# Turning tiles by VectorE's squares of 32 and ScalarE's copies instead of TensorE's transposes, in a hybrid mLSTM and RWKV-7 decoder layer on one core

## The chip, the core and the metric

The kernel runs on one core of a Trainium2 chip. A core has TensorE (PE, matrix products, results in PSUM), VectorE (DVE), ScalarE (ACT), GpSimd (POOL) and SyncE (SP, which here only starts DMAs). The engines run side by side, each through its own list of instructions in order, and wait for one another by semaphores. The metric is the time on the device for one execution, in microseconds (us).

## What is computed

One decoder layer for 256 tokens of width 2048, all in float32. Cut to what matters here:

```python
def hybrid_mixer(h, ...):
    proj = h @ w_in                                   # 2048 -> mLSTM, RWKV and gate columns
    q, k, v, o, ir, fr = split_cols(mlstm_p, MLSTM_COLS)
    hm = mlstm_chunkwise(q, k, v, ig, logf)           # 4 heads, values of 256
    hm = hm * lax.rsqrt(jnp.mean(hm * hm, -1, keepdims=True) + RMS_EPS) * head_norm
    ha = jax.nn.sigmoid(o) * hm
    rp = rwkv_p + (shift_right(rwkv_p, 1) - rwkv_p) * mu
    r, kr, vr, wl, al, gl = split_cols(rp, RWKV_COLS)
    y = rwkv7_scan(r_h, heads(decay), kr, v_h, kk, kk * a_h)   # 16 heads of 64
    y = (y - mean) * lax.rsqrt(var + RWKV_GN_EPS) * per_head(ln_g) + per_head(ln_b)
    y = y + jnp.sum(r_h * kr * r_k, -1, keepdims=True) * v_h
    hb = y.reshape(B, S, RWKV_WIDTH) * g
    merged = sigmoid(g_a) * (ha @ w_branch_a) + sigmoid(g_b) * (hb @ w_branch_b)
    return merged @ w_out

x = x + rms_norm(hybrid_mixer(rms_norm(x)), ...)
x = x + rms_norm(cross_attention(rms_norm(x), rms_norm(mem)), ...)
x = x + rms_norm(conv_glu_ffn(rms_norm(x)), ...)
```

## The kernel before

All large products run through one list of blocks (`block`, `run`). A block is 512 output columns of one weight matrix (1024 in the last). Its weights come in tiles of 512 KB, 128 x 1024 numbers, by SP's queue. Each tile is split in two parts for precision: ScalarE casts it to `wh` (L410), VectorE subtracts to get `wl` (L432), and TensorE makes three products, `xh*wh`, `xl*wh` and `xh*wl`, into PSUM tiles called `fm` (features on partitions) or `tm` (tokens on partitions). A `fm` tile of weights is 24 matmuls of 128x256. There are three buffers for `raw`, four each for `wh` and `wl`.

Counted from 0, tiles 0 to 7 are the small columns, 8 to 71 RWKV's r, k, v and mLSTM's q, k, 72 to 103 mLSTM's v and o as `tm`, 104 to 111 and 112 to 119 the first two gate blocks, then branch and gate blocks in turn (120 to 123 is the first branch block on `ha`, 168 to 171 the first on `hb`), and after them the mixer's output, cross-attention and the feed-forward part, which is most of the span.

All other work is side work, written as Python generators and dealt out between the matmuls by a class `Spread`. `side.half()` is called at every half tile. It runs a piece (up to the next `yield`) of the first bulk generator or of a back one if a budget for VectorE and ScalarE allows it, and a piece of each chain whose turn it is: a chain with `chain=3` comes every third half tile. `side.need(s)` runs a generator to its end at once. Before each block, `run` needs the evacuation of the block before the last:

```python
            if len(pend) >= 2:
                side.need(pend[-2])
```

The order on each engine is fixed by this when the program is built (a manual schedule).

The pieces that the change touches: `gates` (chain of 1) makes mLSTM's gate row `R[6]` and spreads it over 128 partitions by matmuls with a row of the identity (`gbc`, from a split copy `g2`), for `pw`. `v_evac` makes RWKV's v in features (`vT`) and turns it into tokens (`vt`) by TensorE's transposes. `rwkv` (both halves `together`, a chain of 3) runs four chunks of 64 tokens; in chunks 0 to 2 it turns the keys BK into `bkt`, then come the steps gram, lv1 with X, lv2, U, and Tn with Y; after chunks 1 and 3 the outputs are normed (`gm`, `gv`) and turned (`yT`) into `z`. `mlstm`, the tail of the evacuation of the last `o` block, makes its output `so` in tokens and turns it (`haT`) for the split into `ha`. `hb_split` makes `hb` from RWKV's outputs with the products `zg`, whose weights `gwh` and `gwl` it splits twice; `need_hb` needs it before the first branch block on `hb`. `x_tokens`, in the feed-forward part, already turns x by VectorE's transpose of squares of 32 (`xq`) and sixteen ScalarE copies of 32 partitions (`xt`) that put the squares into their places.

Of the kernel before, what the change touches and what calls it, by code (L numbers as in the profile page):

```python
# [9 lines left out]
F32 = mybir.dt.float32  # L10
F32R = mybir.dt.float32r
# [141 lines left out]
def _layer(ctx, tc, nc, d, dbg):  # L153
# [58 lines left out]
    E2 = [slice(0, 64), slice(64, 128)]  # L212
    mhalf = cp.tile([P, 16], F32, name="mhalf")
    pool.memset(mhalf, -0.5)
# [439 lines left out]

    id4 = cp.tile([4, 4], F32R, name="id4")

    def gates():

        act.copy(id4, con[0:4, 0:4])
        RT = M["rows"]  # L660
# [72 lines left out]
        M["pw"] = pw  # L733
        g2 = T2("g2", dt=F32R)
        split(g2[0:4, 0], g2[0:4, 1], R[6])
        for _ in range(6):
            yield
        for h2 in range(2):
            q = aux("gbc", [P, 2, S])
            for j in range(2):  # L740
                sel = id4[:, h2 * 2 + j:h2 * 2 + j + 1].broadcast_to((4, P))
                mm(q[:, j], sel, g2[0:4, 0], stop=False)
                mm(q[:, j], sel, g2[0:4, 1], start=False)
            for j in range(2):
                h = h2 * 2 + j
                for (jt, dq), ci in CI.items():
                    o = jt * 256 + dq * 64 - jt * 128
                    dve.tensor_scalar(pw[:, h, o:o + 64], q[:, j, dq * 64:(dq + 1) * 64], cols[:, ci, h:h + 1], 0.0,
                                      op0=ALU.subtract, op1=ALU.max)
                yield  # L750
# [171 lines left out]
    def v_evac(hf):  # L922
        def gen(ps):
            if hf == 0:
                M["vT"], M["vt"] = U("vT"), U("vt", [P, 2, 1024])
            for g in range(2):
                p0 = hf * 4 + g * 2
                pr = PR()
                dve.tensor_mul(pr, ps[g], bc(st0.rb, 2))
                yield  # L930
                for j in range(2):
                    shiftmix(M["vT"][:, p0 + j], pr[:, j], 16 + p0 + j)
                yield
            for _ in range(4):
                yield
            for t in range(2):
                q = aux("vt", [P, 4, 128])
                for j in range(4):
                    pe.transpose(q[:, j], M["vT"][:, hf * 4 + j, t * P:(t + 1) * P], ident)
                act.copy(M["vt"][:, t, hf * 512:(hf + 1) * 512], q)  # L940
                yield
            M["v", hf] = True
            start_rwkv()
            tasks["bon", hf] = side.add(bonus(hf), back=True)
        return gen

    def bonus(hf):
# [11 lines left out]
    def rwkv(hf):  # L959
# [6 lines left out]
        def heads():  # L966
            for j in range(4):
                for e in range(2):
                    yield j, e

        ysb = None
        for c in range(4):
# [5 lines left out]
            if c < 3:  # L978
                q = aux("bkt", [P, 4, 128])
                for j in range(4):  # L980
                    pe.transpose(q[:, j], flat(BK[:, p0 + j, c]), ident)
                act.copy(bkt, q)
                yield
            au = C("au", f"au{hf}", [P, 2, 2, 4, 64])
# [15 lines left out]
            for e in range(2):  # L1000
                act.copy(uv[E2[1 - e], e], v[:, e])
            yield

# [9 lines left out]
            if c:  # L1013
                q = aux("X0", [P, 4, 64])
                for j, e in heads():
                    mm(q[E2[e], j], KR[E2[e], p0 + j, c, 0], T[hf][E2[e], j])
                for e in range(2):
                    dve.tensor_add(uv[E2[e], e], uv[E2[e], e], q[E2[e]])
            yield
            q = aux("lv2", [P, 4, 32])  # L1020
            for j, e in heads():
                mm(q[e * 64:e * 64 + 32, j], t1[E2[e], j], mt[E2[e], j, 32:64])
            for e in range(2):
                r = slice(e * 64, e * 64 + 32)
                dve.tensor_copy(mt[r, :, 32:64], q[r])
            yield
            q = aux("U", [P, 4, 64])
# [49 lines left out]
            dve.tensor_mul(y, y, r.unsqueeze(2).broadcast_to((P, 8, 64)))  # L1077
            yield
            yield
            q = aux("yT", [P, 4, 128])  # L1080
            for j in range(4):
                pe.transpose(q[:, j], y[:, j * 2:j * 2 + 2].rearrange("p a b -> p (a b)"), ident)
            z = bg[:, 1].rearrange("p (j t) -> p j t", j=4)
            for j in range(4):
                act.activation(z[:, j], q[:, j], AF.Identity, scale=pcol("lng", p0 + j), bias=pcol("lnb", p0 + j))
            yield
# [55 lines left out]
    def mlstm():  # L1142
# [4 lines left out]
        for t in range(2):  # L1147
# [12 lines left out]
            for h2 in range(2):  # L1160
# [19 lines left out]
                yield  # L1180
        ha = [U(f"ha{i}", dt=F32R) for i in range(2)]
        M["ha"] = ha
        for k2 in range(4):
            q = aux("haT", [P, 2, S])
            for j in range(2):
                k = k2 * 2 + j
                for t in range(2):
                    pe.transpose(q[:, j, t * P:(t + 1) * P], so[:, t, k * P:(k + 1) * P], ident)
# [476 lines left out]
    def x_tokens():  # L1665

        M["xt"] = []
        for f in range(4):
            if f % 2 == 0:
                M["xt"].append(U("xt", [P, 2, 1024]))  # L1670
            q = C("xq", f"au{f % 2}", [P, 4, 2, 4, 32])
            flat = q.rearrange("p k t b i -> p (k t b i)")
            for i in range(2):
                v = M["xr"][f // 2][:, f % 2 * 4 + i * 2:f % 2 * 4 + i * 2 + 2]
                dve.transpose(flat[:, i * 512:(i + 1) * 512], v.rearrange("p k s -> p (k s)"))
                yield
            o = M["xt"][f // 2][:, :, f % 2 * 512:f % 2 * 512 + 512].rearrange("p t (k b i) -> p t k b i", k=4, b=4)
            for b in range(4):
                for c in range(4):
                    act.copy(o[b * 32:b * 32 + 32, :, :, c], q[c * 32:c * 32 + 32, :, :, b].rearrange("p k t i -> p t k i"))  # L1680
                    if c % 2:
                        yield

# [157 lines left out]
```

## Time and profile before

| what | value |
|---|---|
| median of 3 runs | 1883.01 us (1882.06 to 1885.18) |
| the profiled execution | 1882.86 us |
| its span in the profile | 1881.1 us |
| TensorE busy | 1867.8 us (99%) |
| VectorE busy | 1313.9 us (70%) |
| ScalarE busy | 1035.0 us (55%) |
| GpSimd busy | 30.6 us (2%) |
| mean granted TensorE clock | 0.997 |

How to read the profile: a row of groups has line, engine, operation, tiles written and read, shapes and count, then the busy time, the mean of one in ns, the idle time of the engine just before, and what ended it. A row of a tile has the count, then the shortest, median and longest duration. A row of the timeline has the start in us, the time from the first start to the last end of the instructions merged in it, the engine, the instruction and their count; in brackets stands idle time before it and its releaser. A row of windows has the stretch, its length, the busy time (and instructions) of PE, PE's weight loads, DVE, ACT and POOL, the granted TensorE clock, and the share and rate of the DMA engines. A row of waits has who waited for whom, total, times, longest. Nearly all operations of the side work are recorded at L66, in a helper that meters them, and plain matmuls at L188.

Matmuls are pipelined: the durations of neighbours overlap, so their distance in the timeline says what one costs in a stream. In some matmul groups a few records are missing.

### The profile page before, as it was taken

To read this page: it belongs to the slowest core of one execution; us is meant where nothing else is said; L and a number is where in the kernel's file an instruction comes from. 1 tells how busy PE (TensorE), PEld (TensorE's weight loads), DVE (VectorE), ACT (ScalarE), POOL (GpSimd) and SP (SyncE) were. 2 spreads that over 40 slices of the span, in tenths; PEclk is the share of its full clock that TensorE was granted. 3 is DMA by queue.
4 is the path that set the end of the run, shared out by engine and by line. 5 is a ranking of instruction groups with operands and counts; after the bars stand their busy time and mean duration, and the time that the engine had idled before them with its cause. 6 is when DMAs were issued, how large, how long until landed. Compare 5 with 4: busy or idle time off the path is not lost.

```text
span 1881.1 us, 36660 instructions
## 1 busy us (share of the span) xinstructions
PE 1867.8 (99%) x15038; PEld 1774.5 (94%) x15038; DVE 1313.9 (70%) x1957; ACT 1035.0 (55%) x1619; POOL 30.6 (2%) x53
## 2 busy tenths in 40 slices
PE   9999999999999999999999999999999999999998
PEld 9999988999999999899999999999999998888886
DVE  6879985765765767777877666777666675556555
ACT  6677355554544655666565555564445555545453
POOL 0000000100100000000000000000000000000000
PEclk9999999999999999999999999999999999999999
DMA  7655554354556664545555566555655556555554
GB/s 252 196 175 181 167 177 146 110 175 146 182 175 206 237 234 163 176 163 180 197 196 192 199 194 198 194 191 191 195 198 193 196 191 216 195 192 196 193 190 154
DMA packets 97912, 352.73 MB, mean 188 GB/s; under 512 B 11056, under 2 KB 11312, under 8 KB 97360
## 3 DMA queue, kind: packets, MB, share of 16 engines
q1 hardware_dynamic: 96496, 348.07, 56.2%
q8 instruction: 117, 1.92, 0.4%
q0 software_dynamic: 384, 1.18, 0.3%
q10 hardware_dynamic: 864, 1.15, 0.2%
q14 instruction: 51, 0.42, 0.1%
HBM read 347.73 MB, written 2.10 MB: 186 GB/s over the span
## 4 chain that ended last, share of the span: by engine, by line
PE 95%; DVE 3%; issue 1%; ACT 1%; DMA 0%; POOL 0%; SPq 0%; DVEq 0%; POOLq 0%; ACTq 0%
PE fm L188 66%; PE tm L188 24%; DVE wl L432 1%; PE gram L188 0%; PE Y L188 0%; DVE ql L66 0%; ACT wh L410 0%; PE lv L188 0%; DMA wsm<-in_w_sm_dram 0%; DVE z L66 0%; PE num L188 0%; DVE hl L66 0%; PE X L188 0%; PE zwa L188 0%; PE U L188 0%
## 5 line engine op out<-in xcount | busy, mean ns | idle before, releaser
L432 DVE TENSOR_TENSOR wl<-raw,wh 128x1024 fp32r<-128x1024 f32 (+2 forms) x756 | 789.3, 1059 | 427.4 <-ACT wh L410 424.3
L410 ACT CAST wh<-raw 128x1024 fp32r<-128x1024 f32 (+2 forms) x756 | 679.8, 916 | 520.7 <-PE fm L188 335.0
L188 PE MATMUL fm<-fh,wl 128*128 128x256 f32 x2048 | 566.3, 277 | 0.5 <-DVE wl L432 0.4
L188 PE MATMUL fm<-fh,wh 128*128 128x256 f32 x2048 | 566.3, 277 | 0.1
L188 PE MATMUL fm<-fl,wh 128*128 128x256 f32 x2048 | 565.0, 276 | 0.0
L188 PEld LDWEIGHTS fm<-fh,wl 128*128 128x128 f32 x2048 | 385.0, 188 | 1.0 <-DVE wl L432 1.0
L188 PEld LDWEIGHTS fm<-fh,wh 128*128 128x128 f32 x2048 | 384.9, 188 | 0.4 <-ACT fh L66 0.4
L188 PEld LDWEIGHTS fm<-fl,wh 128*128 128x128 f32 x2048 | 384.5, 188 | 0.0
L188 PE MATMUL tm<-wh,as 128*128 128x512 f32 x1024 | 315.1, 389 | 0.0
L188 PE MATMUL fm<-hh,wh 128*128 128x256 f32 x1072 | 302.0, 282 | 1.4 <-ACT wh L421 1.4
L188 PE MATMUL fm<-hh,wl 128*128 128x256 f32 x1072 | 298.3, 278 | 0.1
L188 PE MATMUL fm<-hl,wh 128*128 128x256 f32 x1072 | 298.2, 278 | 0.0
L188 PEld LDWEIGHTS tm<-wh,as 128*128 128x128 f32 x1024 | 192.1, 188 | 39.8
L188 PEld LDWEIGHTS fm<-hh,wh 128*128 128x128 f32 x1072 | 202.4, 189 | 3.4 <-ACT hh L66 1.5
L188 PEld LDWEIGHTS fm<-hl,wh 128*128 128x128 f32 x1072 | 202.4, 189 | 0.2
L188 PEld LDWEIGHTS fm<-hh,wl 128*128 128x128 f32 x1072 | 202.3, 189 | 0.3 <-DVE wl L422 0.3
L188 PE MATMUL tm<-wl,as 128*128 128x512 f32 x512 | 199.2, 389 | 0.0
L188 PEld LDWEIGHTS tm<-wl,as 128*128 128x128 f32 x512 | 96.1, 188 | 20.0
L66 ACT CAST as<-ac 128x256 fp32r<-128x256 f32 x128 | 45.6, 404 | 113.5 <-PE tm L188 113.5
L66 DVE TENSOR_TENSOR as<-ac,as 128x256 fp32r<-128x256 f32 x128 | 48.6, 421 | 62.2 <-ACT as L66 62.2
L188 PE MATMUL fm<-mgh,wh 128*128 128x256 f32 x256 | 71.0, 277 | 0.0
L188 PE MATMUL fm<-mgh,wl 128*128 128x256 f32 x256 | 70.9, 277 | 0.0
(361 smaller groups left out, 2156.1 us busy)
## 6 DMA issues: line engine op xcount, KB each, us to landing
raw<-in_w_fu_dram SPq DMA_DIRECT2D x256, 512.0 KB, 4.2
raw<-in_w_in_dram SPq DMA_DIRECT2D x160, 512.0 KB, 3.7
raw<-in_w_fd_dram SPq DMA_DIRECT2D x128, 512.0 KB, 4.0
raw<-in_w_br_dram SPq DMA_DIRECT2D x32, 512.0 KB, 3.9
raw<-in_w_mo_dram SPq DMA_DIRECT2D x32, 512.0 KB, 4.1
raw<-in_w_xk_dram SPq DMA_DIRECT2D x8, 512.0 KB, 4.3
raw<-in_w_xq_dram SPq DMA_DIRECT2D x8, 512.0 KB, 3.6
raw<-in_w_xv_dram SPq DMA_DIRECT2D x8, 512.0 KB, 3.9
```

The lines of the kernel that those rows point to most:

```text
L66: return f(out, *a, **k)
L188: pe.matmul(out, lhsT, rhs, start=start, stop=stop, skip_group_check=True)
L410: nc.scalar.copy(h, v)
L432: nc.vector.tensor_sub(l, v, h)
```

## The change

Four transposes and one spreading by TensorE are replaced. A helper `turned` (taken out of `x_tokens`) and two like it (`squares`, `h_features`) transpose squares of 32 on VectorE and move the squares on ScalarE. v becomes a chain of its own (`v_tokens`, every second half tile); the keys' copies are dealt out, three per half of the heads, over the steps of a chunk; the outputs' copies go four at a time over the recurrence's steps; mLSTM's output goes through an extra tile `hs`, its first token tile as a chain beside the second. The gates' row goes to 128 partitions by four DMAs from POOL's queue into `gb`, with eight turns of waiting instead of six. The T2 tiles get a seventh buffer.

```diff
-        return mp.tile(shape or [P, 2, S], dt, tag="T2", bufs=6, name=name)
+        return mp.tile(shape or [P, 2, S], dt, tag="T2", bufs=7, name=name)
...
+    def turned(q, v, o):
+        n = v.shape[1]
+        flat = q.rearrange("p k t b i -> p (k t b i)")
+        for k in range(0, n, 2):
+            dve.transpose(flat[:, k * S:(k + 2) * S], v[:, k:k + 2].rearrange("p k s -> p (k s)"))
+            yield
+        o = o.rearrange("p t (k b i) -> p t k b i", k=n, b=4)
+        for b in range(4):
+            for c in range(4):
+                act.copy(o[b * 32:b * 32 + 32, :, :, c], q[c * 32:c * 32 + 32, :, :, b].rearrange("p k t i -> p t k i"))
+                if c % 2:
+                    yield
...
-        g2 = T2("g2", dt=F32R)
-        split(g2[0:4, 0], g2[0:4, 1], R[6])
-        for _ in range(6):
+        gb = C("gb", "au1", [P, 4, S])
+        for h in range(4):
+            pool.dma_start(gb[:, h], R[6][h:h + 1].unsqueeze(1).broadcast_to((1, P, S)))
+        for _ in range(8):
             yield
         for h2 in range(2):
-            q = aux("gbc", [P, 2, S])
-            for j in range(2):
-                sel = id4[:, h2 * 2 + j:h2 * 2 + j + 1].broadcast_to((4, P))
-                mm(q[:, j], sel, g2[0:4, 0], stop=False)
-                mm(q[:, j], sel, g2[0:4, 1], start=False)
...
-            for t in range(2):
-                q = aux("vt", [P, 4, 128])
-                for j in range(4):
-                    pe.transpose(q[:, j], M["vT"][:, hf * 4 + j, t * P:(t + 1) * P], ident)
-                act.copy(M["vt"][:, t, hf * 512:(hf + 1) * 512], q)
-                yield
...
+            side.add(v_tokens(hf), chain=2)
...
+        def squares(o, v):
+            q = T2("bq", [P, 4, 4, 32])
+            dve.transpose(q.rearrange("p j b i -> p j (b i)"), v)
+            yield
+            for b in range(4):
+                for a in range(4):
+                    act.copy(o[b * 32:b * 32 + 32, :, a * 32:a * 32 + 32], q[a * 32:a * 32 + 32, :, b])
+                    yield
...
-                q = aux("bkt", [P, 4, 128])
-                for j in range(4):
-                    pe.transpose(q[:, j], flat(BK[:, p0 + j, c]), ident)
-                act.copy(bkt, q)
-                yield
+                turn = squares(bkt, BK[:, p0:p0 + 4, c].rearrange("p j s t -> p j (s t)"))
+                next(turn)
...
+                for _ in zip(range(3), turn):
+                    pass
                 yield
...
-            yield
-            q = aux("yT", [P, 4, 128])
+            z = bg[:, 1].rearrange("p (j t) -> p j t", j=4)
+            turn = squares(z, y.rearrange("p (j e) v -> p j (e v)", e=2))
+            next(turn)
+            yield
+            for n in range(16):
+                next(turn)
+                if n % 4 == 3:
+                    yield
...
+            if t == 0:
+                hs = U("hs", [P, 2, 8, 4, 32])
+                turn0 = side.add(h_features(hs[:, 0], so[:, 0]), chain=1)
+        yield from h_features(hs[:, 1], so[:, 1])
+        side.need(turn0)
...
-            q = aux("haT", [P, 2, S])
             for j in range(2):
                 k = k2 * 2 + j
-                for t in range(2):
-                    pe.transpose(q[:, j, t * P:(t + 1) * P], so[:, t, k * P:(k + 1) * P], ident)
-            for j in range(2):
-                k = k2 * 2 + j
-                split_gain(ha[0][:, k], ha[1][:, k], q[:, j], pcol("hn", k))
+                h, l = (v[:, k].rearrange("p (t s) -> p t s", t=2) for v in ha)
+                split_gain(h, l, sof[:, k], pcol("hn", k))
             yield
+    def h_features(q, v):
+        flat = q.rearrange("p k b i -> p (k b i)")
+        for i in range(2):
+            dve.transpose(flat[:, i * 512:(i + 1) * 512], v[:, i * 512:(i + 1) * 512])
+            yield
+        o = v.rearrange("p (k a i) -> p k a i", k=8, a=4)
+        for b in range(4):
+            for a in range(4):
+                act.copy(o[b * 32:b * 32 + 32, :, a], q[a * 32:a * 32 + 32, :, b])
+                if a % 2:
+                    yield
```

More of the change, by code (lines that the diff above doesn't have):

```diff
@@ L212, in _layer @@
     E2 = [slice(0, 64), slice(64, 128)]
-    mhalf = cp.tile([P, 16], F32, name="mhalf")
+    mhalf = cp.tile([P, 24], F32, name="mhalf")
     pool.memset(mhalf, -0.5)
@@ L933, in gen, with v_tokens @@
                 yield
-            for _ in range(4):
-                yield
-            for t in range(2):
-                q = aux("vt", [P, 4, 128])
-                for j in range(4):
-                    pe.transpose(q[:, j], M["vT"][:, hf * 4 + j, t * P:(t + 1) * P], ident)
-                act.copy(M["vt"][:, t, hf * 512:(hf + 1) * 512], q)
-                yield
-            M["v", hf] = True
-            start_rwkv()
-            tasks["bon", hf] = side.add(bonus(hf), back=True)
-        return gen
+            side.add(v_tokens(hf), chain=2)
+        return gen
+    def v_tokens(hf):
+        for p0 in (hf * 4, hf * 4 + 2):
+            yield from turned(T2("vq", [P, 2, 2, 4, 32]), M["vT"][:, p0:p0 + 2], M["vt"][:, :, p0 * P:p0 * P + 256])
+        M["v", hf] = True
+        start_rwkv()
+        tasks["bon", hf] = side.add(bonus(hf), back=True)
     def bonus(hf):
@@ L978, in rwkv @@
             if c < 3:
[L979 to L983 removed]
+                turn = squares(bkt, BK[:, p0:p0 + 4, c].rearrange("p j s t -> p j (s t)"))
+                next(turn)
+            else:
+                turn = iter(())
             au = C("au", f"au{hf}", [P, 2, 2, 4, 64])
@@ L1001, in rwkv @@
                 act.copy(uv[E2[1 - e], e], v[:, e])
+            for _ in zip(range(3), turn):
+                pass
             yield
@@ L1018, in rwkv @@
                     dve.tensor_add(uv[E2[e], e], uv[E2[e], e], q[E2[e]])
+            for _ in zip(range(3), turn):
+                pass
             yield
@@ L1025, in rwkv @@
                 dve.tensor_copy(mt[r, :, 32:64], q[r])
+            for _ in turn:
+                pass
             yield
@@ L1078, in rwkv @@
             yield
+            z = bg[:, 1].rearrange("p (j t) -> p j t", j=4)
+            turn = squares(z, y.rearrange("p (j e) v -> p j (e v)", e=2))
+            next(turn)
             yield
-            q = aux("yT", [P, 4, 128])
+            for n in range(16):
+                next(turn)
+                if n % 4 == 3:
+                    yield
             for j in range(4):
[L1082 to L1085, printed above, removed]
+                act.activation(z[:, j], z[:, j], AF.Identity, scale=pcol("lng", p0 + j), bias=pcol("lnb", p0 + j))
             yield
@@ L1671, in x_tokens @@
             q = C("xq", f"au{f % 2}", [P, 4, 2, 4, 32])
[L1672 to L1675, printed above, removed]
+            v = M["xr"][f // 2][:, f % 2 * 4:f % 2 * 4 + 4]
+            o = M["xt"][f // 2][:, :, f % 2 * 512:f % 2 * 512 + 512]
+            for _ in turned(q, v, o):
                 yield
[L1677 to L1682, printed above, removed]
     def load_gain():
```

5 lines of the change are left out of this document (2 added, 3 removed).

## The prediction

> **What bounds the kernel now.** I read the page first, then who waited for whom, then the order of time around the places that the change touches.
>
> ```profile
> span 1881.1 us, 36660 instructions
> PE 1867.8 (99%) x15038; PEld 1774.5 (94%) x15038; DVE 1313.9 (70%) x1957; ACT 1035.0 (55%) x1619; POOL 30.6 (2%) x53
> PE 95%; DVE 3%; issue 1%; ACT 1%; DMA 0%; POOL 0%; SPq 0%; DVEq 0%; POOLq 0%; ACTq 0%
> ```
>
> TensorE (PE) is busy for 99% of the span and is 95% of the chain that ended last. So every microsecond taken out of its stream is a microsecond won, as long as nothing else makes it wait. What could is the staging of the weights: ScalarE casts each 512 KB tile (wh), VectorE subtracts (wl), both are in line with all the other work of their engines.
>
> ```profile
> PE fm L188 <- DVE wl L432: 0.4, 1, 0.4
> ACT wh L410 <- PE fm L188: 335.0, 225, 4.0
> ```
>
> In the whole span TensorE waited once for a wl, 0.4 us, while ScalarE waited 335 us for TensorE to free a wh buffer (there are four). The staging runs ahead, and short bursts on ScalarE are hidden.
>
> **What TensorE loses.** The counts, and what a group of four transposes takes out of a stream of matmuls:
>
> ```profile
> L981 PE MATMUL bkt<-con,BK 128*128 128x128 f32 x24 | 3.1, 272 | 0.0
> L939 PE MATMUL vt<-con,vT 128*128 128x128 f32 x16 | 2.4, 273 | 0.0
> L1188 PE MATMUL haT<-con,so 128*128 128x128 f32 x16 | 2.4, 273 | 0.0
> L1082 PE MATMUL yT<-con,ysb 128*128 128x128 f32 x16 | 2.1, 273 | 0.0
> L188 PE MATMUL gbc<-g,id 4*128 4x256 f32 x8 | 1.5, 303 | 0.0
> ```
>
> ```profile
> 343.33 0.28 PE L188 MATMUL fm<-hh,wl 128*128 128x256 f32 x1
> ...
> 343.67 0.28 PE L188 MATMUL fm<-hh,wl 128*128 128x256 f32 x1
> 343.78 0.60 PE L1188 MATMUL haT<-con,so 128*128 128x128 f32 x4
> ...
> 344.47 0.28 PE L188 MATMUL fm<-hh,wl 128*128 128x256 f32 x1
> ```
>
> ```profile
> 83.20 0.28 PE L188 MATMUL fm<-hh,wl 128*128 128x256 f32 x1
> 83.41 0.74 PE L188 MATMUL gbc<-g,id 4*128 4x256 f32 x4
> ...
> 84.42 0.28 PE L188 MATMUL fm<-hh,wl 128*128 128x256 f32 x1
> ```
>
> Three fm matmuls take 343.67 - 343.33 = 0.34 us, so a tile of 24 takes 2.72 us. With four transposes between, the same three take 344.47 - 343.67 = 0.80: the group costs 0.46. There are 24 + 16 + 16 + 16 = 72 transposes, 18 groups: 18 x 0.46 = 8.3 us. A group of four gbc matmuls costs 84.42 - 83.20 - 0.34 = 0.88, two of them 1.8. Off TensorE's stream: **10.1 us**, as every one of these stages is PE-bound.
>
> The duration of a transpose is no price here, since the next matmul starts before it ends. [...]
>
> **What the other engines get.** By the code, 18 VectorE transposes of 128x512, 224 ScalarE copies of 32x128 (v 64, keys 96, outputs 64) and 32 of 32x256 (mLSTM's output). The tokens of x already go this way:
>
> ```profile
> L66 DVE STREAM_TRANSPOSE xq<-xr x8: 702/704/706, 936.3 to 1187.7; 128x512 f32<-128x512 f32 x8
> 948.96 0.82 ACT L66 COPY xt<-xq 32x256 f32<-32x256 f32 x2
> L410 ACT CAST wh<-raw 128x128 fp32r<-128x128 f32 x116 | 34.2, 295 | 0.0
> ```
>
> VectorE: 18 x 0.70 = 12.7 us. A 32x256 copy takes 0.41 us of ScalarE (two in 0.82; they do not overlap): 32 x 0.41 = 13.1. The 32x128 copy is not in the trace; the nearest row is a cast of as many elements, 0.295, and without overlap I take 0.30 (ends 0.20, with the overlap that whole-partition casts have, and 0.41): 224 x 0.30 = 67. Some 80 us more for ScalarE in a stretch of about 400, of which it idles nearly half. Most of it is dealt out at 6 or 8 copies (1.8 to 2.4 us) in a tile whose neighbour has none. A tile of 2.72 us less a cast of 1.05 leaves 1.67, and with four wh buffers a cast can start three tiles (8.2 us) before its use, so a reserve of about 8.2 - 1.05 - 1.23 (cast and subtraction, rows below) = 5.9 us covers this: cost 0, taken as 0.5 (0 to 2) for the steps of the recurrence, whose own matmuls wait for ScalarE more directly.
>
> The gates' row: four DMAs on POOL's queue, ahead of the two of uh.
>
> ```profile
> 81.06 0.71 POOL L624 DMA_DIRECT2D uh<-uh  x1 [12.85 <-ACT uh L66]
> uh<-uh POOLq DMA_DIRECT2D x2, 256.0 KB, 4.4
> ```
>
> POOL idles 12.85 us before uh, because it doesn't wait for the side work's turn but only for the row, which is ready by then. Four issues of 0.7 and 4.4 us of flight end long before the consumer, eight half tiles later. Queued behind are only uh's two DMAs. Cost 0; if the cover were gone, VectorE would wait a few us in front of a wl that has 5.9 us of reserve. The two extra half tiles put the gates' Exp between the Sigmoids of lw: in the built order ScalarE has two table loads more.
>
> ```profile
> L66 ACT ACT_TABLE_LOAD x4 | 5.1, 1283 | 2.9 <-PEq L1833 1.7 <-DVE tg L66 1.3
> ```
>
> 2 x 1.28 = 2.6 us, three tiles apart, inside the same reserve: 0.
>
> **Where it does not stay hidden (A).** h_features makes mlstm's tail 21 pieces instead of 11, at one or fewer per half tile, and the block that follows the next one forces it to its end (run: side.need of the block before the last). In the built order three stretches of 6, 4 and 4 so-copies come in time, and then, at the start of the second gate block (its tiles are 112 to 119), ScalarE has 18 so-copies, the 8 ha activations and one sg in one piece between the casts of tiles 114 and 115; VectorE has the 8 subtractions, an sg and six norm instructions (gm, ysb) ahead of the subtraction of tile 115. Durations:
>
> ```profile
> 102.28 0.91 ACT L66 ACTIVATE BK<-pr,om 128x256 f32<-128x256 f32 x2 [0.65 <-DVE pr L66]
> 355.26 1.06 ACT L410 CAST wh<-raw 128x1024 fp32r<-128x1024 f32 x1
> 359.35 0.68 PE L188 MATMUL Y<-T,KR 64*64 64x64 f32 x16
> 360.07 0.75 ACT L66 COPY ysb<-Y 64x256 f32<-64x256 f32 x2 [0.95 <-PE Y L188]
> 360.84 1.14 ACT L410 CAST wh<-raw 128x896 fp32r<-128x896 f32 x2
> 365.36 1.23 DVE L432 TENSOR_TENSOR wl<-raw,wh 128x1024 fp32r<-128x1024 f32 x1 [1.64 <-ACT wh L410]
> 366.50 0.69 DVE L66 TENSOR_TENSOR sg<-fm,st_b 128x512 f32<-128x512 f32 x1
> 367.10 0.68 DVE L66 TENSOR_REDUCE gm<-ysb 128x8 f32<-128x512 f32 x1
> ...
> 370.16 1.28 DVE L432 TENSOR_TENSOR wl<-raw,wh 128x896 fp32r<-128x896 f32 x2
> ```
>
> Let 0 be the end of chunk 1's Y matmuls. After them TensorE has 9 half tiles (12.2 us) to the second gate block and three tiles more to tile 115: it wants that at 20.4, its wl at 20.6. ScalarE: ysb done at 0.8; the cast of tile 111 waits for tile 107 to end, at 1.4, to 2.3; six copies to 4.8, cast to 5.9, four to 7.5, cast to 8.5, four to 10.2, cast (114) to 11.3; 18 x 0.41 = 7.4 to 18.7; eight ha at 0.41 (two in 0.91, so 0.50 each with 0.09 overlap) to 22.1. VectorE ends the last subtraction 0.5 later, sg 0.6, the norm 370.16 - 367.10 = 3.1, wl 1.2: 27.5. TensorE waits **7 us** (4 if copies overlap like whole casts; 8 if ScalarE comes late).
>
> Such a pause has a second price. At the other place where TensorE pauses:
>
> ```profile
> 820.00:823.00 3.00, 2.17 (x17) 1.95 (x17) 0.16 (x1) 1.72 (x5) 0.70 (x1) 1.00 0.29 113
> 823.00:827.00 4.00, 3.87 (x21) 3.58 (x20) 3.50 (x8) 1.02 (x2) 0.00 (x0) 0.57 0.03 6
> ```
>
> 0.8 us idle in 3, and in the next 4 us the granted clock is 0.57: 4 x 0.43 = 1.7 us lost. I add **1.7** for A (0 to 3.4). [...]
>
> **And (B).** Outputs turned by copies take six steps of the recurrence's chain before the normed output is used instead of two, twice, and the keys save a step three times: 2 x 4 - 3 = 5 steps of three half tiles, 20 us later. In the built order hb_split then has no time left: its last gwh split is forced at the start of the first hb block, and the zg matmuls that need it stand one tile (2.72 us) behind the previous zg.
>
> ```profile
> 501.76 1.78 ACT L66 CAST gwh<-gup 128x512 fp32r<-128x512 f32 x3
> 503.03 0.69 DVE L66 TENSOR_TENSOR gwl<-gup,gwh 128x512 fp32r<-128x512 f32 x1
> 503.75 0.68 DVE L66 TENSOR_TENSOR gwh<-gup,gwh 32x512 fp32r<-32x512 f32 x1
> 511.82 0.62 ACT L66 CAST hb<-vT 128x512 fp32r<-128x512 f32 x1 [1.76 <-DVE vT L66]
> ```
>
> From the end of that previous zg: vT product 0.7, hb cast 0.6 (1.3), a tile's cast to 2.4, its wl to 3.6, gwl to 4.3, gwh to 5.0. TensorE is there at 2.7, and its first matmuls, 0.3 us, need less: **2.0** (0.5 to 3), and 0.8 for the clock (0 or 1.7).
>
> **Sum.** The profiled execution took 1882.86 us, its span 1881.1; the median of the three runs is 1883.01, 0.15 more. 1882.86 - 10.1 + 0.5 + 7.0 + 1.7 + 2.0 + 0.8 = **1884.8 us**: the gain is spent on two pauses that the change itself makes. 0.2%, what the measurement can tell, is 3.8 us; this is 1.8 above the median, no change.
>
> **Rivals.** First, faster by the duration: 72 x 0.273 + 8 x 0.303 = 22.1 us off, the pauses as above: 1872.8. The stream around haT speaks against it. 0.02. Second, faster because A is small: the copies overlap (0.31 instead of 0.41: 18 x 0.1, and no lateness of 0.7 before them, 2.5 less), the clock stays, B is 1: 1882.86 - 10.1 + 4.5 + 1.0 = 1878.3. [...] 0.16. Third, slower: ScalarE becomes the bound inside the recurrence. In the step before lv1, X waits for the second half's copies from vt, behind six copies from vt and the keys' squares: 4 x 0.41 + 3 x 0.30 = 2.5 us of ScalarE against a step of 3 x 1.36 = 4.1. From 1.6 us of lateness on, which one cast and one step's rest already bring, TensorE pays each further one; at 1 us in two steps of three chunks it is 6 us: 1890.8. For it speak stretches of 3.5 us in a row, against it that the recurrence's own matmuls lengthen those tiles. 0.32, together with A or B at their dear ends (1884.8 + 1.0 + 1.7 + 1.0 + 0.9 = 1889.4). The forecast keeps 0.50.
>
> **Numbers.** Faster by over 0.2% (under 1879.2) 0.18, within 0.50, slower (over 1886.8) 0.32. The range goes from the second rival to the third, 1878.0 to 1891.0; the forecast's own range is 1880.5 to 1887.
>
> **What would show it.** Right: no transposes on TensorE but xpT's; a single wait of fm for wl of 5 to 8 us in the second gate block, with half clock behind it; a wait of zg for gwh of some 2 us; elsewhere hardly a wait. Wrong: copies of 32x256 that start 0.31 apart; waits of lv or X for ScalarE's au copies adding to several us; a wait of DVE pw for the DMA; or a span 8 us and more shorter with no pause.

## The result, and the profile after

| kernel | median (us) | range | ratio to before |
|---|---|---|---|
| before | 1883.6 | 1882.1 to 1885.2 | |
| changed | 1911.05 | 1909.5 to 1915.1 | 1.0149, 95% interval 1.0133 to 1.0165 |

The change makes the kernel 28 us slower. The forecast was 1884.8 us with a range up to 1891.0: wrong, and by much. The profiled execution took 1911.61 us. First its page (span and busy times) and, from the waits over the whole span, three rows on the weights.

```profile
span 1909.8 us, 36786 instructions
PE 1870.0 (98%) x14958; PEld 1773.8 (93%) x14958; DVE 1321.1 (69%) x1974; ACT 1110.8 (58%) x1865; POOL 34.6 (2%) x57
```

```profile
ACT wh L410 <- DMA raw<-in_w_in_dram: 54.8, 26, 18.5
...
PE fm L188 <- ACT wh L410: 13.4, 2, 8.9
...
PE fm L188 <- DVE wl L432: 4.7, 5, 2.1
```

TensorE idles 1909.8 - 1870.0 = 39.8 us, before 1881.1 - 1867.8 = 13.3: **26.5 us more**. Before, it waited once for one of these weights, 0.4 us; now 13.4 + 4.7 = 18.1 us, and one cast of ScalarE waited 18.5 us for its load from memory. That is a wait which the prediction did not have at all.

**Where it happened.** The DMA view of 60 to 95 us in the changed kernel, then in the kernel before, and the landing times of the row `gb` from its tile's view:

```profile
q0 software_dynamic: 192, 0.52, 48.1%
...
raw<-in_w_in_dram SPq DMA_DIRECT2D x6, 512.0 KB, 11.8
gb<-rows POOLq DMA_DIRECT2D x4, 128.0 KB, 14.1
```

```profile
q0 software_dynamic: 160, 0.52, 7.7%
...
raw<-in_w_in_dram SPq DMA_DIRECT2D x12, 512.0 KB, 4.0
```

```profile
L748 POOL DMA_DIRECT2D gb<-rows x4: 536/542/740, 65.0 to 66.8; - x4
...
DMA to landing us min/median/max: 7.3/14.1/19.6
```

POOL's queue (q0) moves the same 0.52 MB as before (`gb` now, `uh` then), but its packets hold the 16 DMA engines for 48.1% of the stretch instead of 7.7%. In the same 35 us 6 weight tiles are issued instead of 12, and they take 11.8 us instead of 4.0. The first of the four DMAs lands at 65.0 + 7.3 = 72.3 us, the last at 66.8 + 19.6 = 86.4: 14.1 us for three times 128 KB, 4.7 each, 28 GB/s. When the last has landed, the starved cast starts (timeline of ScalarE), and the windows show what TensorE did meanwhile (columns as before: PE's busy time behind the length, then PEld, DVE, ACT, POOL, granted clock, DMA):

```profile
86.84 1.04 ACT L410 CAST wh<-raw 128x1024 fp32r<-128x1024 f32 x1 [18.52 <-DMA raw<-in_w_in_dram]
```

```profile
75.00:80.00 5.00, 4.02 (x36) 3.81 (x34) 0.00 (x0) 0.00 (x0) 0.00 (x0) 1.00 1.01 61
80.00:85.00 5.00, 0.00 (x0) 0.00 (x0) 0.00 (x0) 0.00 (x0) 0.00 (x0) 0.71 0.89 86
85.00:90.00 5.00, 1.60 (x5) 1.30 (x6) 2.09 (x4) 1.86 (x3) 0.00 (x0) 0.50 0.54 217
90.00:95.00 5.00, 5.00 (x36) 5.00 (x36) 3.19 (x8) 4.31 (x9) 0.53 (x1) 0.77 0.56 142
```

0.98 + 5.0 + 3.4 = 9.4 us without work. The half clock (a granted clock of 0.50 from 82.1 to 92.3 us) costs where there is work: 1.60 x 0.50 + 5.00 x 0.23 = 2.0 us.

**The two pauses that were forecast** are there. A, ScalarE's timeline and the windows:

```profile
374.02 1.14 ACT L410 CAST wh<-raw 128x896 fp32r<-128x896 f32 x2
375.19 7.46 ACT L66 COPY so<-hs 32x256 f32<-32x256 f32 x18
382.68 3.30 ACT L66 ACTIVATE ha<-so,par 128x256 fp32r<-128x256 f32 x8
...
387.67 1.03 ACT L410 CAST wh<-raw 128x1024 fp32r<-128x1024 f32 x1
```

```profile
384.00:388.00 4.00, 0.22 (x2) 0.01 (x1) 3.93 (x11) 2.85 (x7) 0.00 (x0) 1.00 0.00 0
388.00:392.00 4.00, 1.16 (x5) 0.96 (x6) 3.82 (x6) 0.78 (x2) 0.00 (x0) 0.66 0.00 0
392.00:396.00 4.00, 4.00 (x21) 4.00 (x21) 2.56 (x5) 4.00 (x7) 0.42 (x1) 0.50 0.50 148
```

The 18 copies and 8 activations stand between two casts as the built order said, 0.41 us each (7.46 / 18), not overlapping. TensorE idles 3.78 + 2.84 = 6.6 us (forecast 7.0), 4.5 of it for the cast of a tile and 2.1 for its wl, where the prediction had one wait for the wl; the half clock behind costs 1.16 x 0.34 + 4.00 x 0.50 = 2.4 (forecast 1.7). B, the longest wait of zg and the windows:

```profile
PE zg L188 <- ACT gwh L66: 1.3, 1, 1.3
```

```profile
564.00:570.00 6.00, 3.58 (x26) 3.00 (x25) 4.48 (x7) 3.32 (x6) 0.00 (x0) 1.00 0.44 127
570.00:575.00 5.00, 5.00 (x32) 5.00 (x31) 3.27 (x5) 1.23 (x2) 0.00 (x0) 0.66 0.18 70
```

6.00 - 3.58 = 2.4 us of waiting (forecast 2.0) and 5 x 0.34 = 1.7 of half clock (forecast 0.8). Where v's tokens and the keys are turned, forecast at 0.5 us, TensorE loses more: 1.5 + 0.75 + 1.7 = 3.9 us between 160 and 300 us, and 2.5 in one wait of X near 445 us (timeline of ScalarE below the windows):

```profile
160.00:200.00 40.00, 38.49 (x337) 38.29 (x336) 36.61 (x59) 32.20 (x65) 6.17 (x4) 1.00 0.51 160
200.00:250.00 50.00, 49.25 (x442) 44.62 (x442) 48.75 (x86) 27.00 (x52) 2.22 (x4) 1.00 0.53 169
250.00:300.00 50.00, 48.32 (x297) 40.04 (x296) 39.97 (x68) 36.74 (x74) 0.00 (x0) 1.00 0.58 179
```

```profile
442.32 0.91 ACT L66 COPY bg<-bq 32x128 f32<-32x128 f32 x3
443.25 2.08 ACT L410 CAST wh<-raw 128x1024 fp32r<-128x1024 f32 x3
445.36 0.27 ACT L66 COPY m<-lv 128x128 f32<-128x128 f32 x1
```

The recurrence itself starts at 279 us, with its first `gram`. The 2.2 us before that are waits for a wl (1.5 and 0.5) and for `qk` (0.2), beside the copies of v. In the recurrence X waits 1.7 us at 297 us, for VectorE's `vT`, and 2.5 us near 445 us, for ScalarE's `m`. X does not read `m`. By the code it takes the PSUM buffer (one of the four of `aux`) that this copy empties, and it starts at 445.68, as the copy ends; the copy stands behind three copies of keys and the casts of two tiles.

### The profile page after: what moved, and what is told of

It is laid out like the page before. It is cut to its first block, busy times and chain, and to the rows that moved or that the text cites. A ratio compares the mean times of both kernels' runs of the same rounds, so it can differ in the third digit from the quotient of the medians.

```text
span 1909.8 us, 36786 instructions
## 1 busy us (share of the span) xinstructions
PE 1870.0 (98%) x14958; PEld 1773.8 (93%) x14958; DVE 1321.1 (69%) x1974; ACT 1110.8 (58%) x1865; POOL 34.6 (2%) x57
## 4 chain that ended last, share of the span: by engine, by line
PE 90%; DVE 4%; ACT 3%; DMA 2%; issue 1%; POOL 0%; DVEq 0%; POOLq 0%; SPq 0%; ACTq 0%
PE fm L188 63%; PE tm L188 23%; DVE wl L432 2%; DMA raw<-in_w_in_dram 1%; ACT wh L410 1%; ACT bg L66 1%; ACT so L66 0%; PE gram L188 0%; PE Y L188 0%; PE num L188 0%; DVE BK L66 0%; PE X L188 0%; DMA wsm<-in_w_sm_dram 0%; DVE tmp L66 0%; PE lv L188 0%
## 5 line engine op out<-in xcount | busy, mean ns | idle before, releaser
L188 PE MATMUL fm<-hh,wh 128*128 128x256 f32 x1072 | 304.2, 284 | 14.6 <-ACT wh L410 13.4
```

The costliest lines, as they stand in the source:

```text
L188: pe.matmul(out, lhsT, rhs, start=start, stop=stop, skip_group_check=True)
```

## The experiments

Each kernel was measured on one chip together with the kernel before, whose medians are 1882.8 to 1883.9 us. The kernels that turn v, the keys or the recurrence's outputs have the seventh T2 buffer as well.

| label | median (us) | ratio to before, 95% interval |
|---|---|---|
| row_alone | 1899.8 | 1.0089 (1.0074 to 1.0104) |
| all_but_row | 1902.0 | 1.0096 (1.0081 to 1.0111) |
| row_via_dram | 1884.2 | 1.0002 (0.9993 to 1.0012) |
| row_on_sp | 1896.6 | 1.0067 (1.0048 to 1.0085) |
| row_two_hops | 1882.1 | 0.9996 (0.9987 to 1.0004) |
| row_16_same | 1891.2 | 1.0050 (1.0034 to 1.0067) |
| row_16_ports | 1882.2 | 0.9996 (0.9987 to 1.0006) |
| after_row_via_dram | 1900.1 | 1.0091 (1.0077 to 1.0105) |
| mlstm_alone | 1892.4 | 1.0055 (1.0038 to 1.0072) |
| mlstm_half | 1892.0 | 1.0038 (1.0024 to 1.0052) |
| outputs_alone | 1896.6 | 1.0072 (1.0057 to 1.0087) |
| outputs_compact | 1899.1 | 1.0085 (1.0068 to 1.0103) |
| outputs_two_steps | 1898.1 | 1.0075 (1.0060 to 1.0089) |
| outputs_first | 1885.2 | 1.0012 (1.0004 to 1.0021) |
| tokens_keys_alone | 1885.6 | 1.0014 (1.0005 to 1.0024) |
| tokens_alone | 1885.4 | 1.0007 (0.9998 to 1.0016) |
| keys_alone | 1891.3 | 1.0036 (1.0023 to 1.0049) |
| transposes_twice | 1891.0 | 1.0044 (1.0030 to 1.0058) |

**The row, alone and left out.** row_alone is the kernel before with the `gates` part of the diff only; all_but_row is the changed kernel without it.

> The kernel before with one part of the change alone: the gates' row spread by four DMAs. Theory (row): in the changed kernel's profile the casts run 2.6 us ahead of the kernel before at 65 us and 13.8 us behind it at 130 us, so this stretch costs 16.4 us, and the four DMAs alone are to blame: 1883.6 + 16.4 = 1900 (1896 to 1902). Rival (ScalarE): the delay there belongs to the load of ScalarE and its tables, and the row's DMAs are hidden as forecast: 1883.6 - 1.8 of matmuls = 1882 (1881 to 1884).

> The changed kernel with the gates' row by TensorE's matmuls again. Theory (row): 1911 - 16.4 = 1894.6 (1892 to 1898), with no wait of a weight cast for its load above a few us at 65 to 90 us. Rival (ScalarE): the delay stays and the matmuls come back, 1911 + 1.8 = 1913 (1909 to 1914).

row_alone is 17 us slower, as the theory has it, with the same wait:

```profile
ACT wh L410 <- DMA raw<-in_w_in_dram: 27.8, 6, 19.4
...
PE fm L188 <- ACT wh L410: 10.4, 1, 10.4
```

The ScalarE rival is out: here no tile is turned, and ScalarE has but the four Exp in other places and two table loads more, which row_two_hops below has too and loses nothing. all_but_row confirms the direction but not the size, 9 us instead of 16.4. Its trace lacks the pause at 80 us altogether; against that it is 2 us later than the changed kernel by 30 us, long before any part of the change, and has two stretches of half clock more, 1.7 us each, one of them at 32 us (its mean granted clock is 0.993, that of the changed kernel, with the pause, 0.992). The parts do not add up, here nor below.

**What about the row costs.** Three other ways for the same 512 KB, all on row_alone:

```diff
 row_via_dram
-            pool.dma_start(gb[:, h], R[6][h:h + 1].unsqueeze(1).broadcast_to((1, P, S)))
+        pool.dma_start(dr, R[6])
+            pool.dma_start(gb[:, h], dr[h:h + 1].broadcast_to((P, S)))
 row_on_sp
+            sp.dma_start(gb[:, h], R[6][h:h + 1].unsqueeze(1).broadcast_to((1, P, S)))
 row_two_hops
+            pool.dma_start(gb[0:16, h], R[6][h:h + 1].unsqueeze(1).broadcast_to((1, 16, S)))
+        for k in range(16, P, 16):
+            pool.dma_start(gb[k:k + 16], gb[0:16])
```

> As row_alone, but the row's four heads (4 KB) are first stored to a scratch tensor in the chip's memory, and the four DMAs of 128 KB spread them from there, on POOL's queue as before; the gates' piece yields ten half tiles instead of eight. Theory (source): what costs is that 128 reads of 1 KB come from one partition; from memory they land in a few us, as the broadcast load of gain does (1024 KB in 7.4 us): 1882.8 - 1.8 of matmuls + 0 to 2 = 1882 (1880 to 1885). Rival (queue): the descriptors of POOL's software queue are the cost, 1899 (1896 to 1902).

> As row_alone, but the four DMAs are issued on SP's hardware queue, among the loads of the weights. Theory (source): one partition is read as before, so as slow or, since the loads stand behind them in the same queue, slower: 1900 (1897 to 1910). Rival (queue): the time goes with POOL's queue: 1882 (1880 to 1885).

> As row_alone, but the row goes first to 16 partitions (four DMAs of 16 KB) and from these by seven DMAs of 64 KB to the other 112, all on POOL's queue inside SBUF. Theory (one partition): the reads of one partition fall to an eighth, and what is read from 16 partitions goes as fast as uh (256 KB in 4.4 us): 1882 to 1887. Rival (SBUF as source of a broadcast): 1896 to 1902.

The DMA rows of the three, in this order (KB each, median us to landing); for row_on_sp two waits as well:

```profile
gb<-dr POOLq DMA_DIRECT2D x4, 128.0 KB, 6.1
```

```profile
gb<-rows SPq DMA_DIRECT2D x4, 128.0 KB, 15.8
```

```profile
ACT wh L410 <- DMA raw<-in_w_in_dram: 25.6, 4, 19.4
...
PE zwa L188 <- DMA uh<-uh: 8.8, 1, 8.8
```

```profile
gb<-gb POOLq DMA_DIRECT2D x7, 64.0 KB, 5.0
gb<-rows POOLq DMA_DIRECT2D x4, 16.0 KB, 2.3
```

The queue is not it: on SP's the DMAs take as long (15.8 us to landing, on POOL's 14.6 in row_alone) and the weights wait as long (19.4 us at most in both; the kernel loses 13 us, a little less than its theory's range). The source is: from memory (6.1 us a DMA), or from 16 partitions (2.3 and 5.0), the same bytes cost nothing that can be measured. No kernel shows the 1.8 us of matmuls as a gain: the intervals of row_two_hops and row_16_ports (below) hold both that and nothing, and that of row_via_dram leaves it out.

**Partition or path.** The four DMAs come from four partitions, and still land one after another (from 72.3 to 86.4 us in the changed kernel). Two kernels deal them out in sixteen pieces, the four heads in turn:

```diff
 row_16_same
+        for k in range(0, P, 32):
+            for h in range(4):
+                pool.dma_start(gb[k:k + 32, h], R[6][h:h + 1].unsqueeze(1).broadcast_to((1, 32, S)))
 row_16_ports
+            pool.dma_start(gp[h * 4:h * 4 + 1], R[6][h:h + 1])
+                pool.dma_start(gb[k:k + 32, h], gp[h * 4:h * 4 + 1].unsqueeze(1).broadcast_to((1, 32, S)))
```

> As row_alone, but each head's row is spread in four DMAs of 32 partitions (32 KB), the four heads in turn, still from partitions 0 to 3; twelve half tiles of waiting. Theory (neighbours share a path): four neighbouring partitions together give the 28 GB/s of one, so 512 KB still take some 19 us and hold up the loads: 1896 to 1902. Rival (each partition for itself): in turn they are read side by side, 512 KB in some 5 to 8 us: 1882 to 1886. [...]

> As row_16_same, but four small DMAs (1 KB each) first bring the heads' rows to partitions 0, 4, 8 and 12, and the sixteen DMAs read them there. Theory (neighbours share a path): now four paths are read side by side, 512 KB in some 5 to 8 us, and the loads wait little: 1882 to 1887. Rival (each partition for itself): as row_16_same, whatever that gives; a third (each DMA's one source is what counts, side by side or not): both 1896 to 1902.

```profile
gb<-rows POOLq DMA_DIRECT2D x16, 32.0 KB, 10.1
```

```profile
gb<-gp POOLq DMA_DIRECT2D x16, 32.0 KB, 3.9
```

The same pieces in the same order: 10.1 us each from partitions 0 to 3, 3.9 from 0, 4, 8 and 12. Between 55 and 110 us q0's packets hold the 16 DMA engines for 29.7% in row_16_same and for 10.4% in row_16_ports, with 1.05 MB in both. So it counts here where the source partitions lie, and the theory that neighbours share a path fits where its rivals do not; what that path is, no run shows. At the 4.7 us of the trace for 128 KB, 28 GB/s, 512 KB over one path would take 18.8 us, an estimate. That row_16_same came out at 1891 instead of 1896 to 1902 is a miss of the time alone: as small pieces the row lets more of the weights past (a cast waits 4.4 us at most for its load, in row_alone 19.4), so TensorE waits 2.7 us for a cast instead of 10.4.

**The whole change with the row mended.**

> The changed kernel with the row's four heads stored to a scratch tensor in the chip's memory and spread from there. Theory (source): as all_but_row less 1.8 of matmuls, 1900 (1898 to 1903), with no wait of a cast for a load of weights above 5 us at 65 to 95 us. Rival (the row was half of it): only part of the 9 us comes back, 1905 (1903 to 1909).

As the theory has it; between 55 and 110 us no cast waits more than 3.3 us for its load. 17 us remain of which the row has no part.

**mLSTM's output (A).** mlstm_alone is the kernel before with the `h_features` part; mlstm_half turns only the first token half so:

```diff
+        yield from side.patience(turn0, 6)
+                pe.transpose(q[:, j], so[:, 1, k * P:(k + 1) * P], ident)
+                split_gain(ha[0][:, k, 0:P], ha[1][:, k, 0:P], so[:, 0, k * P:(k + 1) * P], pcol("hn", k))
+                split_gain(ha[0][:, k, P:S], ha[1][:, k, P:S], q[:, j], pcol("hn", k))
```

> The kernel before with mLSTM's output alone turned by squares and copies. In the built order the burst of 18 so-copies and 8 ha activations between the casts of tiles 114 and 115 is there as in the changed kernel. Theory (burst): the delay grows there by the 8 us that it grew by in the changed kernel (16 to 24), gain included: 1883.6 + 8 = 1891.6 (1889 to 1894), with half clock behind the pause. Rival (load): the burst hurts because the keys' and the outputs' copies leave ScalarE no reserve there; alone it costs as much as it gains: 1883.6 (1881 to 1886).

> The kernel before with the first token half of mLSTM's output turned by squares and copies and the second by TensorE; the tail waits up to six pieces for the copies to be dealt out. In the built order the casts of tiles 112, 113, 114 and 115 have 4 copies, 4 copies, 8 copies and 8 activations, and 8 activations ahead of them: 1.6, 1.6, 5.7 and 2.4 us of ScalarE. Theory (reserve): what stays within 5.9 us and 1.7 a tile costs nothing, so no pause, and two groups of transposes gained: 1883.2 - 0.9 = 1882.3 (1880 to 1884). Rival (load): each copy has its price, so half of the 9.5 us of mlstm_alone: 1888 (1886 to 1890).

mlstm_alone is as the burst theory has it in kind: 4.7 us of waiting and 2.6 of half clock at the burst, and no other copies are added to ScalarE there. That the time fits too is in part luck, since its trace also waits 3.1 us at `xsc`, at 780 us, far behind the burst, where before waited 0.7. mlstm_half is a miss, 1892.0, beyond both ranges: the casts come in time now, but TensorE waits all the same, in the recurrence (a matmul of TensorE, two instructions of VectorE, then windows):

```profile
359.52 0.69 PE L188 MATMUL Tn<-au,bg 128*64 128x64 f32 x16 [1.17 <-DVE ha L66]
```

```profile
359.12 0.35 DVE L66 SCALAR_TENSOR_TENSOR ha<-haT,par,ha 128x128 fp32r<-128x128 f32 x1 [0.17 <-ACT ha L66]
...
365.74 0.41 DVE L66 TENSOR_TENSOR T<-T,Tn 128x256 f32<-128x256 f32 x1
```

```profile
360.00:365.00 5.00, 3.37 (x56) 2.80 (x52) 4.04 (x13) 3.81 (x11) 0.00 (x0) 0.60 0.27 75
365.00:370.00 5.00, 4.78 (x46) 4.49 (x45) 3.08 (x7) 3.14 (x6) 0.00 (x0) 0.50 0.08 33
```

`Tn` does not read `ha`. It starts when the subtraction that empties the first `haT` ends, at 359.12 + 0.35 = 359.47, while the state's additions come only at 365.74. By the code `Tn`, `Y` and `haT` share four PSUM buffers (`aux`), and the four `haT` hold all of them until ScalarE and VectorE have made `ha` of them; the other three waits of Tn and Y end in the same way. This is read from the order of times and was not tried apart. So the reserve of 5.9 us is one of the weights; the recurrence's own steps have less. The 3 us of idle time cost 4 more by the clock: 3.37 x 0.40 + 4.78 x 0.50 and a rest behind.

**The first recurrence's outputs (B).** outputs_alone is the kernel before with the `squares` of y; the other three change how they are dealt out:

```diff
 outputs_compact (no pieces), outputs_two_steps (n == 7)
             for n in range(16):
                 next(turn)
-                if n % 4 == 3:
-                    yield
 outputs_first
+            if tt == 0:
+                turn = squares(z, y.rearrange("p (j e) v -> p j (e v)", e=2))
...
+            else:
+                    pe.transpose(q[:, j], y[:, j * 2:j * 2 + 2].rearrange("p a b -> p (a b)"), ident)
```

> The kernel before with the first recurrence's outputs alone turned by squares and copies. In the built order hb_split then ends at the last tile before the first hb block, with 3 gwh and 4 hb pieces ahead of one cast, more than in the changed kernel. Theory (late hb): the delay grows at about 540 to 560 us by the 6 us that it grew by in the changed kernel, gain included: 1883.6 + 6 = 1889.6 (1887 to 1893). Rival (as forecast): 2.8 us lost less 1.8 gained, 1884.6 (1883 to 1886).

> As outputs_alone, but the 16 copies of an output are one step with the four activations behind them, so the recurrence has as many steps as before, and in the built order hb_split comes where it came before. Theory (late hb): the pause of zg goes, and the cost with it: 1882.8 - 8 x 0.23 of transposes + 0 to 2 = 1882 (1880 to 1885). Rival (load): the copies themselves are what TensorE waits for, now in one piece of 5 us: 1893 to 1898 as in outputs_alone.

> As outputs_alone, but the 16 copies of an output are dealt out in two steps of 8, so that both halves together put 4.8 us into one half tile, and hb_split keeps its distance from the first hb block (its last pieces stand ahead of tile 167). Theory (reserve): pieces within the reserve are hidden, and the pauses of outputs_alone and of outputs_compact were the forced end of hb_split and a piece beyond it: 1883.2 - 1.8 + 0 to 2 = 1882.5 (1880 to 1885). Rival (load): 128 more copies between two gate blocks are too many however they are dealt out: 1893 to 1899.

> The kernel before with the outputs of the first token half alone (two of the four) turned by squares and copies in four steps each, those of the second half by TensorE. In the built order hb_split then keeps its own spacing, with its last pieces ahead of tile 170. Theory (late hb): zg waits under 0.5 us and no delay grows at 540 us; 1896.6 less the pause and its half clock (4.8 + 2.8) is 1889 (1886 to 1891). Rival (load): the copies cost by their number, so half of outputs_alone's 13.7, with half of its growth, some 5 us, still at 540 us: 1890.7 (1889 to 1893).

The waits that matter, of outputs_alone, outputs_compact and outputs_two_steps, and ScalarE's timeline of the last:

```profile
PE zg L188 <- ACT gwh L66: 3.3, 1, 3.3
```

```profile
PE fm L188 <- ACT wh L410: 9.9, 2, 6.4
```

```profile
PE fm L188 <- ACT wh L410: 9.7, 2, 5.1
```

```profile
380.16 4.92 ACT L66 COPY bg<-bq 32x128 f32<-32x128 f32 x16
385.10 1.14 ACT L410 CAST wh<-raw 128x896 fp32r<-128x896 f32 x2
...
388.65 2.45 ACT L66 COPY bg<-bq 32x128 f32<-32x128 f32 x8
...
396.82 1.03 ACT L410 CAST wh<-raw 128x1024 fp32r<-128x1024 f32 x1
```

outputs_alone has the late hb, and more of it than the changed kernel, but it is a miss in size: 13.6 us slower, where its theory had 6. At zg its trace has 4.7 us of waiting and 2.8 of half clock; X waits 1.4 us with 1.7 of half clock at 430 us, and `xsc` 2.4 us; the rest is not accounted for. outputs_compact and outputs_two_steps keep hb in time, and zg waits no more, but both lose as much at another place: at a block's end the two halves' copies and activations stand together, in outputs_two_steps 4.9 us and, from 388.65 to 396.82, 8.2 us, with one cast between. The expectation of outputs_two_steps counted the copies of a step and forgot the eight activations (3.3 us) behind the second. outputs_first, with half the copies, in slow steps, is 2.3 us slower; zg has no wait in it. That is less than both theories gave, and its longest wait in the recurrence is X's 1.4 us. So the late hb makes the pause at zg, shown by its going. That the copies cost elsewhere because they come in heaps, and not by their number, is argued from these pauses: outputs_first has both half the copies and slow steps.

**Tokens and keys.** The kernel before with `v_tokens`, with the keys' `squares`, and with both.

> The kernel before with v's tokens and the keys alone turned by squares and copies. Theory (bound, the third rival of the prediction): the waits inside the recurrence cost more than the ten groups of transposes gain; in all_but_row the delay grows from 2.0 to 4.4 us between 150 and 320 us: 1882.8 + 2.4 = 1885 (1883 to 1888). Rival (hidden, as forecast): 10 x 0.46 gained, 0.5 lost, 1878.7 (1877 to 1881).

> The kernel before with v's tokens alone turned by squares and copies (each half of them a chain of its own ahead of the recurrence's start). Theory (bound): in tokens_keys_alone the delay grows by 2.2 us between 150 and 160 us, where the tokens of the second half are turned beside the first steps: 1883.2 + 2.2 = 1885.4 (1884 to 1887). Rival (hidden, as forecast): four groups of transposes gained: 1881.4 (1880 to 1883).

> The kernel before with the keys alone turned by squares and copies. Theory (bound): in tokens_keys_alone the delay after 160 us ends where it was, so the waits in the recurrence give back what the six groups gain: 1883.2 + 0.2 = 1883.4 (1882 to 1885). Rival (hidden, as forecast): 1883.2 - 2.8 + 0.3 = 1880.7 (1879 to 1882).

Both together cost 2.6 us, the tokens nothing that can be told from the kernel before, and the keys by themselves 6.8, more than with the tokens beside them and a miss of both ranges. In keys_alone X and lv wait for `m`, 330 to 500 us:

```profile
PE X L188 <- ACT m L66: 3.2, 2, 1.7
...
PE lv L188 <- DVE m L66: 2.7, 1, 2.7
```

followed by half clock (a granted clock of 0.66 in 400 to 410 us). With the tokens as a chain of their own the recurrence starts at another half tile, and its steps stand beside other work. That this makes the difference is only argued; it was not tried apart.

**The price of a transpose.** Each `pe.transpose` of the four kinds issued twice, `for j in (0, 1, 2, 3) * 2`.

> The kernel before with each of the 72 transposes of vt, bkt, haT and yT issued twice into the same place, nothing else. Theory (stream price, the prediction's): 18 more groups at 0.46: 1883.9 + 8.3 = 1892 (1890 to 1894). Rival (partly hidden): TensorE waits for other things near these transposes, so a group more or less costs about half of that, as the two profiles suggest: 1888 (1886 to 1890).

1.0044 is 8.3 us (5.6 to 10.9), for 18 groups 0.46 each: the prediction's price. TensorE idles 1888.8 - 1874.6 = 14.2 us in it, before 13.3, and its mean granted clock is 0.999, so it is the price in a stream and no pause.

## Why the prediction was wrong

**The gates' row was put at 0. This is the step that failed.** "Four issues of 0.7 and 4.4 us of flight" took the landing time of uh, whose 256 KB come from 64 partitions, for a transfer that reads 128 times the same 1 KB. And "queued behind are only uh's two DMAs" looked at POOL's queue alone and not at the weights on SP's, whose tiles took 11.8 us instead of 4.0 while q0's packets held the 16 DMA engines for 48.1% of the stretch. In their place the trace shows 128 KB in 4.7 us and the loads of the weights starved. It cost 9.4 us of waiting, 1.9 at zwa behind it, 2.0 of half clock, and 1.7 in a second stretch of it at 123 us: 15.0. The wait at zwa and the second stretch are in row_alone too (2.0 and 1.7), and neither before nor in row_via_dram. The price "if the cover were gone" was asked for VectorE's wait for `gb`, which never came; nobody asked it for the weights.

**Tokens, keys and the recurrence were put at 0.5 and cost 8.1**: 3.9 and 2.5 of waiting and 1.7 of half clock at 447 us. 2.2 of it come ahead of the recurrence, where the prediction put the copies of v at nothing; tokens_alone has such waits for a wl too (0.9 and 0.5). 5.9 are X's. The third rival priced X's waits at 6, but it had X wait for the second half's copies of v. Measured are 2.5 for a PSUM buffer that a copy empties, behind keys and casts on ScalarE, with 1.7 of half clock, and 1.7 for VectorE. So ScalarE's line was seen rightly, the object of the wait was not, and that the sizes meet is luck.

**A and B** were right in place and kind: A 6.6 + 2.4 = 9.0 against 8.7, B 2.4 + 1.7 = 4.1 against 2.8.

**The gain**, 10.1, stands for the transposes by themselves: the 8.3 of the 72 is what doubling them costs. The 1.8 of the gbc matmuls no run shows. In the changed kernel less of the gain is seen. The costs above make 15.0 + 8.1 + 9.0 + 4.1 = 36.2. The profile of before lists 1.7 us of half clock near 823 us, which this one has not. It lists as much at the start, and there the changed kernel has none listed, but its first matmuls are just as far apart, 0.21 us, twice their later distance:

```profile
8.50 0.41 PE L188 MATMUL fm<-hh,wh 128*128 128x256 f32 x1
8.71 0.41 PE L188 MATMUL fm<-hl,wh 128*128 128x256 f32 x1
```

The span grew by 28.7, so 36.2 - 1.7 - 28.7 = 5.8 is all that was gained by this sum. The other 4.3 are lost where TensorE shows as busy, or the profiles differ by so much for other reasons. That stays open. With the four sizes in its places the prediction's own sum, gain included, would be 1884.8 + 15.0 + 7.6 + 0.3 + 1.3 = 1909.0, against the profiled 1911.61; the 1.7 and the 4.3, which it leaves out, partly cancel.

**The rivals.** Faster by the duration of a transpose: out, 0.46 a group stands. A small because copies overlap: out, 18 in 7.46. ScalarE as the bound in the recurrence: there in part, 4.2 of its 6, beside the row. The copies of 32x128 took 0.296 (0.30 forecast).

Left open: why the parts alone, 16.8 + 10.4 + 13.6 + 2.6, make 43 us and together 28, and why the row gives back only 10 to 11 us by the ratios when it is taken out of the whole change or mended there; part of it is that the late hb is smaller in the whole change (4.1 us against 4.7 of waiting and 2.8 of half clock in outputs_alone), and that mlstm_alone and outputs_alone have a pause of 3.1 and 2.4 us at `xsc`, far behind the change, with half clock behind it, that others have shorter.

No version beat the kernel before. The two best, row_two_hops and row_16_ports, are level with it.

## What to carry to other kernels

Before a DMA that spreads one row is put at nothing, ask what it reads: here 128 KB read from one partition took 4.7 us, pieces from four neighbouring ones 10.1 where those from partitions four apart took 3.9, and the loads of the weights, on another queue, 11.8 instead of 4.0. Price each burst of copies together with everything else that the same engine has in line up to the next cast, both halves and their activations included, and against the nearest consumer: the recurrence's own steps have less reserve than the weights (in mlstm_half they waited 3 us where the casts came in time). Ask of each piece also which PSUM buffer it keeps from the next matmul. And where TensorE is the bound, add to a pause of some microseconds the half clock that may come with it, here 1.7 to 4 us where it came.

## What the hardware showed

128 KB from one partition landed in 4.7 us (28 GB/s, from the first and the last landing above). 32 KB pieces took 10.1 us from four neighbouring partitions and 3.9 from partitions four apart. From SP's queue the four DMAs of the row took 15.8 us to landing, from POOL's 14.6 (row_alone). In the changed kernel half clock (a granted clock of 0.50) came in stretches of 3.4, 6.8 and 10.2 us: 10.2 from within the wait of 8.9 on, 6.8 from within A's pause on, 3.4 at 123, 447 and 570 us. It came also at a wait of only 1.4 us in outputs_alone (a granted clock of 0.86 in 430 to 440 us), but not at each longer one: after X's 1.7 us at 297 us, in the changed kernel, the granted clock is 1.00 up to A's pause. outputs_first has a wait of X of 1.4 us too, and a mean granted clock of 0.998 over its span, where outputs_alone has 0.996. What decides whether half clock comes, no run here shows.
